# A gated linear recurrence: its inner levels in blocks of 32 tokens instead of 128 x 128 products

## The chip, the cores and the metric

The program runs on one core of a Trainium2 chip. The metric is the device time of one execution in microseconds, the median of several runs. TensorE is called PE, VectorE DVE, ScalarE ACT, GpSimd POOL, and SyncE, which issues the DMAs, SP.

## The reference, cut to what matters

The reference is a decoder trunk of two layers on 512 tokens of width 1024. Each layer is half a feed-forward step, a mixer, and half a feed-forward step. The second layer's mixer is HGRN2, a linear recurrence with a decay for each key channel, 8 heads of 128 key and 128 value channels. Its heart:

```python
q = jax.nn.silu(zq)
log_f = jnp.logaddexp(jnp.log(lbf), jnp.log1p(-lbf) + jax.nn.log_sigmoid(zf))
k = (1.0 - lbf) * jax.nn.sigmoid(-zf)
...
    bcum = jnp.cumsum(gc, axis=2)
    diff = jnp.where(causal, bcum[:, :, :, None, :] - bcum[:, :, None, :, :], -jnp.inf)
    a = jnp.einsum('bhtk,bhsk,bhtsk->bhts', qc, kc, jnp.exp(diff))
    o_intra = jnp.einsum('bhts,bhsv->bhtv', a, vc)
```

So for each head a causal matrix `a[t, s]` is wanted, the sum over channels of query t times key s times the decay between them, and the output is that matrix times the values (the state that the reference carries from chunk to chunk is the same sum for more distant tokens).

## The kernel before

The decay between two tokens can't be written as a product of one factor per token over long distances without overflow, so the kernel splits the pairs of tokens by distance. The 512 tokens are 4 chunks (`c`) of 128. Pairs in different chunks come from the six products `ai` (lines 1147 to 1155). Pairs within a chunk come from seven levels, `HL` = 64, 32, 16, 8, 4, 2, 1: at the level m a chunk is cut into blocks of 2m, and a pair belongs to the level where its key is in the first half of a block and its query in the second half of the same one. The tile `E` holds, for each level and token, the exponential of the decay between the token and the middle of its block; lines 1167 to 1173 multiply it in place by the keys in the first halves and by the queries in the second halves, one DVE instruction of 256 elements for each half (the two of the level 1 on POOL). Then PE multiplies keys by queries. The diagonal (a token with itself) has no decay.

Which products run is the point of this case. The diagonal is computed as four full products of 128 keys by 128 queries (line 1164), of which DVE keeps the diagonal by a product with the identity (line 1165), writing all of the tile `a`. The level 64 is four products of 64 by 64 (line 1177), the level 32 eight of 32 by 32 (line 1180), alternating chunk by chunk, the level 16 sixteen of 16 by 16 (line 1189), and ACT copies their blocks into `a` (lines 1181, 1183, 1191). The levels 8, 4, 2 and 1 are four products of 128 by 128 each (line 1196): almost all of their output is thrown away, and DVE picks what belongs to the level through a mask of bytes, 512 elements an instruction (line 1197). Each fp32 product is two records on PE, each a load of weights and a pass of the moving operand; such a load and pass is called a pair below. A product whose output has 32 or fewer rows uses only the columns of the array above those PSUM partitions, so products for different partitions can run beside each other.

Eight heads run one after the other, software-pipelined: while the head h is in `hgrn_pairs`, the exponentials of h + 1 are made (line 1109, 1110, 1118, 1119; `EXP_AT` says after which step), the output of h - 1 is formed (`hgrn_out`), and that of h - 2 is transposed and split for the output projection (`hgrn_ot`). PE's instructions stay in the order in which the code is written; the other engines' order is chosen by a scheduler, and each runs its own list in that order. After the last head comes the output projection: `out_proj` loads eight weight tiles `hgrn_w_out` (512 KB each) through the three buffers called `raw`, splits each into `whi` on ACT and `wlo` on DVE, and multiplies. Its PSUM banks: six for the chunks 0 to 2, one each for the transposes of the heads 6 and 7, and the last two, for the chunk 3, are those of the transposes again once `oth` and `otl` have been read from them.

## Time and profile before

| what | value |
|---|---|
| time before, median of 3 runs (lowest to highest) | 2070.39 us (2069.94 to 2071.92) |
| the profiled execution, its own time | 2072.93 us |
| its span in the trace | 2071.2 us |
| the recurrence in the trace (queries' last product to the output projection's first) | 1565.7 to 1675.7 us |
| one head in the middle of it | 13.22 us |

The span is what the trace covers, from the first instruction to the last; the execution's own time is 1.7 us longer. In the trace matmul ends are modelled, so that the durations of neighbouring matmuls overlap; what one costs in a stream is the distance from its start to the next start.

### The profile page before, as it was taken

Reading aid. Unit: us, or ns where it says so; the run is one execution under the profiler, and the core shown is the slowest. Engines: PE = TensorE matmul, PEld = TensorE weight load, DVE = VectorE, ACT = ScalarE, POOL = GpSimd, SP = SyncE. Lnnn points to the kernel's source line nnn. Section 1 sums busy time; section 2 is a strip of 40 time slices with the busy share of each in tenths; the row PEclk is TensorE's granted clock in tenths of the full one; section 3 lists DMA queues with packets and bytes.
Section 4 is the critical chain, followed back from the end, with each engine's and each line's share of the span. In section 5 each row is a group of like instructions: output and inputs, shape, how many; then the busy total and the mean of one; then the engine's idle time right before and its main releaser. Section 6 shows DMA issues by size and latency. Waiting matters only on the chain.

```text
span 2071.2 us, 34517 instructions
## 1 busy us (share of the span) xinstructions
PE 2039.3 (98%) x14265; PEld 1870.6 (90%) x14265; DVE 1402.0 (68%) x2108; ACT 987.2 (48%) x1594; POOL 196.1 (9%) x307
## 2 busy tenths in 40 slices
PE   9999999999999999999999999999999999999998
PEld 9998998978898899899899989988888989998996
DVE  8846865377775896487598568663647869945864
ACT  5543552355565355245345435534736734542551
POOL 0000002001122200000110000020321212000002
PEclk9999999999999999999999999999999999999999
DMA  5441342341101145133234413513230023442331
GB/s 183 123 146 58 103 143 74 91 111 42 31 32 52 61 123 163 41 104 112 91 102 134 142 51 103 175 51 102 88 113 32 2 72 96 128 144 62 102 123 41
DMA packets 138762, 194.00 MB, mean 94 GB/s; under 512 B 8571, under 2 KB 117435, under 8 KB 138604
## 3 DMA queue, kind: packets, MB, share of 16 engines
q1 hardware_dynamic: 138604, 191.79, 29.9%
q8 instruction: 112, 1.84, 0.4%
q14 instruction: 46, 0.38, 0.1%
HBM read 189.58 MB, written 2.19 MB: 93 GB/s over the span
## 4 chain that ended last, share of the span: by engine, by line
PE 82%; DVE 10%; ACT 3%; DMA 2%; issue 1%; POOL 1%; SPq 1%; POOLq 0%; DVEq 0%; ACTq 0%
PE ps L140 22%; PE ps L142 22%; PE ps L141 22%; PE po L860 3%; DVE wlo L124 2%; PE ps L844 2%; DVE raw L394 2%; DMA fr<-in_ffn_w_up_dram 2%; PE ps L1196 1%; PE ps L363 1%; DVE xlo L124 1%; PE sc L811 1%; PE sc L812 1%; PE ps L182 1%; DVE fr L394 1%
## 5 line engine op out<-in xcount | busy, mean ns | idle before, releaser
L124 DVE TENSOR_TENSOR wlo<-raw,whi 128x1024 fp32r<-128x1024 f32 (+1 forms) x253 | 311.4, 1235 | 259.6 <-ACT whi L123 258.7
L123 ACT ACTIVATE whi<-raw 128x1024 fp32r<-128x1024 f32 (+1 forms) x253 | 265.7, 1055 | 337.4 <-PE ps L142 152.8
L140 PE MATMUL ps<-xh,whi 128*128 128x256 f32 (+1 forms) x992 | 294.6, 297 | 1.9 <-DVE qs L754 1.3
L141 PE MATMUL ps<-xl,whi 128*128 128x256 f32 (+1 forms) x992 | 293.4, 296 | 0.7 <-DVE xl L124 0.7
L142 PE MATMUL ps<-xh,wlo 128*128 128x256 f32 (+1 forms) x992 | 293.3, 296 | 0.0
L142 PE MATMUL ps<-whi,xlo 128*128 128x512 f32 x704 | 274.4, 390 | 1.5 <-DVE xlo L124 1.5
L140 PE MATMUL ps<-whi,xhi 128*128 128x512 f32 x704 | 274.5, 390 | 0.0
L141 PE MATMUL ps<-wlo,xhi 128*128 128x512 f32 x704 | 274.0, 389 | 0.0
L140 PEld LDWEIGHTS ps<-xh,whi 128*128 128x128 f32 x992 | 186.6, 188 | 9.6 <-DVE qs L754 1.4
L141 PEld LDWEIGHTS ps<-xl,whi 128*128 128x128 f32 x992 | 186.4, 188 | 7.6 <-DVE xl L124 1.1
L142 PEld LDWEIGHTS ps<-xh,wlo 128*128 128x128 f32 x992 | 186.9, 188 | 6.4
L123 ACT ACTIVATE whi<-fr 128x1024 fp32r<-128x1024 f32 x120 | 126.1, 1061 | 115.5 <-PE ps L141 82.3
L140 PE MATMUL ps<-xh,xhi 128*128 128x256 f32 x640 | 178.0, 278 | 1.6 <-DVE c L449 1.4
L142 PE MATMUL ps<-xh,xlo 128*128 128x256 f32 x640 | 177.6, 278 | 0.0
L141 PE MATMUL ps<-xl,xhi 128*128 128x256 f32 x640 | 177.6, 278 | 0.0
L124 DVE TENSOR_TENSOR wlo<-fr,whi 128x1024 fp32r<-128x1024 f32 x120 | 145.5, 1220 | 45.8 <-ACT whi L123 45.6
L142 PEld LDWEIGHTS ps<-whi,xlo 128*128 128x128 f32 x704 | 132.1, 188 | 30.6 <-DVE xlo L124 3.2
L394 DVE TENSOR_TENSOR raw<-fr 128x1024 f32<-128x1024 f32 x120 | 145.6, 1221 | 17.7 <-DMA fr<-in_ffn_w_up_dram 16.3
L141 PEld LDWEIGHTS ps<-wlo,xhi 128*128 128x128 f32 x704 | 132.2, 188 | 27.1
L140 PEld LDWEIGHTS ps<-whi,xhi 128*128 128x128 f32 x704 | 132.2, 188 | 26.8
L124 DVE TENSOR_TENSOR xlo<-h,xhi 128x1024 fp32r<-128x1024 f32 x44 | 53.9, 1226 | 110.8 <-ACT xhi L123 110.8
L140 PEld LDWEIGHTS ps<-xh,xhi 128*128 128x128 f32 x640 | 120.4, 188 | 2.4 <-DVE c L449 2.4
(270 smaller groups left out, 4830.8 us busy)
## 6 DMA issues: line engine op xcount, KB each, us to landing
raw<-in_ffn_w_down_dram SPq DMA_DIRECT2D x88, 512.0 KB, 3.6
fr<-in_ffn_w_gate_dram SPq DMA_DIRECT2D x80, 512.0 KB, 4.0
fr<-in_ffn_w_up_dram SPq DMA_DIRECT2D x80, 512.0 KB, 5.1
raw<-in_hgrn_w_in_dram SPq DMA_DIRECT2D x32, 512.0 KB, 4.1
raw<-in_nsa_w_in_dram SPq DMA_DIRECT2D x18, 512.0 KB, 4.2
raw<-in_ffn_w_gate_dram SPq DMA_DIRECT2D x8, 512.0 KB, 5.4
raw<-in_ffn_w_up_dram SPq DMA_DIRECT2D x8, 512.0 KB, 4.6
raw<-in_nsa_w_out_dram SPq DMA_DIRECT2D x8, 512.0 KB, 3.5
```

The costliest lines, as they stand in the source:

```text
L123: a = self.nc.scalar.activation(hi, src, AF.Copy)
L124: b = self.nc.vector.tensor_tensor(lo, src, hi.bitcast(F32), op=ALU.subtract)
L140: mm(out, l[0], r[0], start=start, stop=False)
L141: mm(out, l[0], r[1], start=False, stop=False)
L142: mm(out, l[1], r[0], start=False, stop=stop)
L182: self.nc.tensor.transpose(p[:, j, :], self.x[c][:, k * P : (k + 1) * P], self.ident)
L363: nc.tensor.matmul(out, l, xx, start=k == low == 0 and xx is x[0], stop=k == 7 and low == 1)
L394: tt(out, x, y, op=op)
L811: nc.tensor.matmul(sc, l, kh[g][:, ts[0] : ts[0] + x, :n], start=True, stop=False)
L812: nc.tensor.matmul(sc, l, kl[g][:, ts[0] : ts[0] + x, :n], start=False, stop=True)
L844: nc.tensor.transpose(p[:, j * P : j * P + P], pf[:, (b0 + j) * P : (b0 + j + 1) * P], self.ident)
L860: nc.tensor.matmul(po[:, ii, t, :], pt[:, t * (i + 1) + j, :], v[j][:, t, g, :], start=j == 0, stop=j == i)
```

## The change

The diagonal and the levels 16 to 1 are computed in compact blocks of `BD` = 32 tokens: for each level sixteen products of 32 keys by the 16 queries of the same block (line 1208 of the new file), and for the diagonal sixteen of 32 by 32 (line 1172). Two levels share one PSUM bank, 64 columns each. DVE collects them in a small tile `diag` of 128 x 128 elements with masks of that form, 64 elements an instruction, and ACT copies `diag` into `a` by four instructions at the end. `a` is one of two tiles that POOL fills with zeros once. The four products of the level 64 are written in turn to the two halves of the PSUM partitions and stand together, and the eight of the level 32 behind them. At the level 1 the keys are used as they are, since their decay there is one; its queries are multiplied on DVE, and POOL multiplies nothing any more. Keys and queries of a head lie in one tile `kq`, so that one DVE instruction of 512 elements serves a level. `tot` is dropped. The tile `ai` comes from the pool `raw` instead of its own.

```diff
-ON_POOL = ((6, 0), (6, 1))
+BD = 32
...
+            eye = work.tile([P, BD], F32, name="eye")
+            for b in range(0, P, BD):
+                self.nc.gpsimd.tensor_copy(eye[b : b + BD], self.ident[b : b + BD, b : b + BD])
...
+                within = [att.tile([P, NT, P], F32, name=f"a{i}") for i in range(2)]
+                for t in within:
+                    self.nc.gpsimd.memset(t, 0.0)
...
-        tot = att.tile([P, 2], F32, name="tot", bufs=2)
-        dve.tensor_copy(tot, EI[:, 1:4:2, P - 1])
...
-        ai = att.tile([P, 6, P], F32, name="ai", bufs=2)
+        ai = self.raw.tile([P, 6, P], F32, name="ai", tag="raw")
...
+        diag = att.tile([P, NT, BD], F32, name="diag", bufs=2)
+        ps = self.psum()
+        for c, b in blocks:
+            s = slice(c * P + b, c * P + b + BD)
+            mm(ps[b : b + BD, BD * c : BD * c + BD], k[:, s], q[:, s], start=True, stop=True)
+        dve.tensor_tensor(diag, ps[:, 0 : NT * BD].rearrange(four, c=NT), eye.unsqueeze(1).to_broadcast([P, NT, BD]), op=ALU.mult)
+        other(2)
+
+        for l, m in enumerate(HL[:-1]):
+            e = E[:, l].rearrange("p c t -> p (c t)").rearrange("p (b x m) -> p b x m", x=2, m=m)
+            dve.tensor_tensor(e, e, self.ap(kq, 0, [[2 * m, T // (2 * m)], [T + m, 2], [1, m]]), op=ALU.mult)
+
+        e = E[:, 6].rearrange("p c t -> p (c t)")[:, 1::2]
+        dve.tensor_tensor(e, e, q[:, 1::2], op=ALU.mult)
...
-        for l in range(3, 7):
-            other(l + 1)
-            p = self.psum()
-            for c in range(NT):
-                mm(p[:, c * P : c * P + P], E[:, l, c, :], E[:, l, c, :], start=True, stop=True)
-            dve.copy_predicated(a, masks[:, l - 3, :].unsqueeze(1).to_broadcast([P, NT, P]), p.rearrange("p (c t) -> p c t", c=4))
+        for pair in ((2, 3), (4, 5), (6,)):
+            p, copies = self.psum(), []
+            for n, l in enumerate(pair):
+                if l > 2:
+                    other(l + 1)
+                m, at = HL[l], n * T // 2 // NT
+                e = E[:, l].rearrange("p c t -> p (c t)")
+                ev = e.rearrange("p (d b x m) -> p d b x m", d=T // BD, x=2, m=m)
+                for c, b in blocks:
+                    s, o = c * P + b, at + BD // 2 * c
+                    mm(p[b : b + BD, o : o + BD // 2], (k if m == 1 else e)[:, s : s + BD], ev[:, s // BD, :, 1, :], start=True, stop=True)
...
+                copies.append(partial(dve.copy_predicated, to, mask, p[:, at : at + T // 2 // NT].rearrange("p (c b m) -> p c b m", c=NT, m=m)))
+            for f in copies:
+                f()
+        for b in range(0, P, BD):
+            act(a[b : b + BD, :, b : b + BD], diag[b : b + BD], AF.Copy)
```

On PE, in the middle of one head, before: the last products of the level 32, the level 16, exponentials of the next head (lines 1118 and 1109), the levels 8, 4 and 2, exponentials, the level 1.

```order
L1180 MATMUL ps<-E 32x32 x2
L1189 MATMUL ps<-E 16x16 x16
L1118 MATMUL ps<-sums,hl 128x128 x2
L1118 MATMUL ps<-sums,hl 128x256 x2
L1109 MATMUL pa<-sums,hl 128x448 x2
L1196 MATMUL ps<-E 128x128 x12
L1109 MATMUL pa<-sums,hl 128x448 x2
L1196 MATMUL ps<-E 128x128 x4
```

And in the changed kernel, from the diagonal to the last level (line 1126 is the old 1118, 1117 the old 1109):

```order
L1172 MATMUL ps<-kq 32x32 x16
L1117 MATMUL pa<-sums,hl 128x448 x2
L1186 MATMUL ps<-E 64x64 x4
L1190 MATMUL ps<-E 32x32 x8
L1208 MATMUL ps<-E 32x16 x16
L1126 MATMUL ps<-sums,hl 128x128 x2
L1126 MATMUL ps<-sums,hl 128x256 x2
L1117 MATMUL pa<-sums,hl 128x448 x2
L1208 MATMUL ps<-E 32x16 x48
L1117 MATMUL pa<-sums,hl 128x448 x2
L1208 MATMUL ps<-E,kq 32x16 x16
```

The exponentials of the next head stand at the same places between the levels as before; what stands between them are now runs of 16 to 48 small products.

On SP, from the last loads of the queries' weights to those of the next feed-forward step, before:

```order
L132 DMA raw<-in_hgrn_w_in_dram 128x4x256 x4
L132 DMA raw<-in_hgrn_w_out_dram 128x1024 x7
L211 DMA hlg<-in_ln_gain_dram 128x1024
L212 DMA hlb<-in_ln_bias_dram 128x1024
L132 DMA raw<-in_hgrn_w_out_dram 128x1024
L132 DMA raw<-in_ffn_w_gate_dram 128x4x256 x2
```

And in the changed kernel:

```order
L133 DMA raw<-in_hgrn_w_in_dram 128x4x256 x4
L133 DMA raw<-in_hgrn_w_out_dram 128x1024 x4
L212 DMA hlg<-in_ln_gain_dram 128x1024
L213 DMA hlb<-in_ln_bias_dram 128x1024
L133 DMA raw<-in_hgrn_w_out_dram 128x1024 x4
L133 DMA raw<-in_ffn_w_gate_dram 128x4x256 x2
```

The loads have the same order but for three that stand behind `hlg` and `hlb`; but `raw` now belongs to eight tiles `ai` first, one for each head, and a load waits for PE's last use of one of them.

On DVE, from the last head's use of its output (`zg`) to the first normalisation of the output projection, before:

```order
L1216 SCALAR_TENSOR_TENSOR zg_14318<-ps,ry,zg_14318 128x128
L124 TENSOR_TENSOR wlo<-raw,whi 128x1024 x5
L124 TENSOR_TENSOR otl<-ps,oth 128x512 x2
L124 TENSOR_TENSOR wlo<-raw,whi 128x1024 x3
L229 SCALAR_TENSOR_TENSOR x_71<-x_71,ps 128x512
```

And in the changed kernel (one more `wlo`, that of the first output weight, stands ahead of the last two heads' `zg`):

```order
L1234 SCALAR_TENSOR_TENSOR zg_14310<-ps,ry,zg_14310 128x128
L125 TENSOR_TENSOR wlo<-raw,whi 128x1024 x6
L125 TENSOR_TENSOR ot<-ps,ot 128x512
L125 TENSOR_TENSOR wlo<-raw,whi 128x1024 x2
L125 TENSOR_TENSOR ot<-ps,ot 128x512
L125 TENSOR_TENSOR wlo<-raw,whi 128x1024 x3
L230 SCALAR_TENSOR_TENSOR x_71<-x_71,ps 128x512
```

Four more splits of weights stand here, and the split of the head 7's transposed output is behind all eight output weights and the first one of the feed-forward step.

## Rows read from the trace of the kernel before

**Rows 1.** the profile's page, part 1: engine, busy time, share of the span, instructions.

```profile
PE 2039.3 (98%) x14265; PEld 1870.6 (90%) x14265; DVE 1402.0 (68%) x2108; ACT 987.2 (48%) x1594; POOL 196.1 (9%) x307
```

**Rows 2.** busy time by stretch, columns in line one; last: one head.

```profile
core 0: us, PE busy (x) PEld busy (x) DVE busy (x) ACT busy (x) POOL busy (x), PEclk, DMA share, GB/s
1566.00:1571.00 5.00, 3.21 (x18) 2.39 (x16) 0.80 (x3) 4.97 (x8) 0.00 (x0) 1.00 0.33 105
1571.00:1576.00 5.00, 4.66 (x24) 4.47 (x24) 4.53 (x11) 3.64 (x7) 2.08 (x2) 0.66 0.00 0
1576.00:1581.00 5.00, 5.00 (x81) 4.34 (x80) 4.27 (x10) 4.24 (x11) 0.00 (x0) 1.00 0.01 3
1636.06:1649.28 13.22, 13.22 (x150) 12.41 (x150) 11.95 (x29) 8.60 (x24) 3.42 (x5) 1.00 0.01 1
```

**Rows 3.** chain of waits, that head, 13.22 us: shares by line.

```profile
by line: PE ps L1196 27.0%; PE pa L1109 12.2%; PE ps L1154 10.5%; PE ps L1208 10.1%; PE ps L1118 8.1%; PE ps L1177 7.8%; PE ps L1209 6.8%; PE ps L1164 6.7%; PE ps L1180 5.4%; PE ps L1222 3.3%; PE ps L1189 2.0%
```

**Rows 4.** order of time, PE, head before: start, us, line, op, shape, records.

```profile
1626.27 0.33 PE L1177 MATMUL ps<-E 128*64 128x64 f32 x2
1626.53 0.26 PE L1180 MATMUL ps<-E 128*32 128x32 f32 x4
1627.93 0.42 PE L1189 MATMUL ps<-E 128*16 128x16 f32 x29
1628.28 0.73 PE L1118 MATMUL ps<-sums,hl 128*128 128x128 f32 x4
```

**Rows 5.** source lines, PE's sequencer: ns, first and last start (us).

```profile
L1189 PEldq EVENT_SEMAPHORE  x1: 51/51/51, 1627.0 to 1627.0; - x1
L1196 PEldq EVENT_SEMAPHORE  x1: 51/51/51, 1628.5 to 1628.5; - x1
```

**Rows 6.** groups by line, the head of Rows 3: count, busy us, mean ns.

```profile
L1197 DVE COPY_PREDICATED a<-masks,ps 128x512 f32<-128x512 uint8 x4 | 3.0, 742 | 0.0
L1173 DVE TENSOR_TENSOR E<-E,qt 128x256 f32<-128x256 f32 x6 | 2.5, 417 | 0.0
L1165 DVE TENSOR_TENSOR a<-ps,ident 128x512 f32<-128x512 f32 x1 | 0.7, 679 | 0.0
L1139 DVE COPY tot<-EI 128x2 f32<-128x2 f32 x1 | 0.2, 169 | 0.6 <-ACT EI L1119 0.6
L1183 ACT ACTIVATE a<-ps 32x128 f32<-32x128 f32 x2 | 0.5, 260 | 0.0
L1191 ACT ACTIVATE a<-ps 16x64 f32<-16x64 f32 x4 | 0.9, 215 | 0.1
```

**Rows 7.** order of time: DMA issues, DVE and PE around the projection's start.

```profile
1530.02 35.46 SPq L132 DMA_DIRECT2D raw<-in_hgrn_w_out_dram  x7
1682.12 1.51 SPq L132 DMA_DIRECT2D raw<-in_ffn_w_gate_dram  x2
raw<-in_hgrn_w_out_dram SPq DMA_DIRECT2D x7, 512.0 KB, 3.5
1678.70 1.13 DVE L1216 SCALAR_TENSOR_TENSOR zg<-ps,ry,zg 128x128 f32<-128x128 f32 x4 [1.16 <-POOL ry L219]
1679.75 3.48 DVE L124 TENSOR_TENSOR wlo<-raw,whi 128x1024 fp32r<-128x1024 f32 x3
1689.62 1.28 DVE L124 TENSOR_TENSOR otl<-ps,oth 128x512 fp32r<-128x512 f32 x2
1675.67 0.23 PE ps L140
1684.04 0.44 PE ps L1222 x4
1688.66 0.44 PE ps L1222 x4
```

**Rows 8.** line 1154, first head (order of time) and later one (chain).

```profile
1571.35 2.82 PE L1154 MATMUL ps<-qi,ki 128*128 128x128 f32 x12 [0.43 <-DVE ki L1143]
1636.47 1.39 PE ps L1154 x12
```

More of the change, by code (lines that the diff above doesn't have):

```diff
@@ L930, in hgrn_body @@
         w = self.a["hgrn_w_in"][0]
-        kt, qt, xh, xl = [], [], [], []
-        for _ in range(NK):
-            kt.append(pool.tile([P, T], F32, name="kt", tag="kq", bufs=2 * NK))
-            qt.append(pool.tile([P, T], F32, name="qt", tag="kq", bufs=2 * NK))
+        xh, xl = [], []
+        kq = [pool.tile([P, 2, T], F32, name="kq", tag="kq", bufs=NK) for _ in range(NK)]
+        kt, qt = ([t[:, i] for t in kq] for i in range(2))
         zg = [pool.tile([P, D], F32, name=f"zg{c}") for c in range(NT)]
@@ L941, in hgrn_body @@
             sums = work.tile([P, NSUM], F32R, name="sums")
-            masks = work.tile([P, 4, P], U8, name="masks")
+            masks = work.tile([P, 5, BD], U8, name="masks")
+            eye = work.tile([P, BD], F32, name="eye")
+            for b in range(0, P, BD):
+                self.nc.gpsimd.tensor_copy(eye[b : b + BD], self.ident[b : b + BD, b : b + BD])
             with ExitStack() as e2:
@@ L967, in hgrn_body @@
                         *nxt, side = self.hgrn_exps(att, right, self.hgrn_split(parts, h + 1, lf), sums)
-                    last, cur = cur, self.hgrn_pairs(att, h, exps, kt, qt, masks, side)
+                    last, cur = cur, self.hgrn_pairs(att, within[h % 2], exps, kq[h], masks, eye, side)
                     if h > 1:
@@ L1076, in hgrn_proj @@
             pool.tensor_tensor(z3, z3, gn.unsqueeze(1).to_broadcast([P, 4, P]), op=ALU.mult)
-        raw = self.raw.tile([P, 4, P], I32, name="raw", tag="raw")
+        raw = self.raw.tile([P, 5, BD], I32, name="raw", tag="raw")
         nc.sync.dma_start(raw, self.a["masks"])
@@ L1122, in hgrn_exps, with hgrn_pairs @@
         return E, EI, [partial(within, n) if n < NT else partial(across, n - NT, far[n - NT]) for n in EXP_ORDER]
-    def hgrn_pairs(self, att, h, exps, kt, qt, masks, side):
+    def hgrn_pairs(self, att, a, exps, kq, masks, eye, side):
         nc = self.nc
         act, dve, mm = nc.scalar.activation, nc.vector, nc.tensor.matmul
-        k, q = kt[h], qt[h]
+        k, q = kq[:, 0], kq[:, 1]
         E, EI = exps
@@ L1157, in hgrn_pairs @@
         other(1)
-        a = att.tile([P, NT, P], F32, name="a", bufs=2)
-        af = a.rearrange("p c t -> p (c t)")
+        blocks = [(c, b) for c in range(NT) for b in range(0, P, BD)]
+        four = "p (c t) -> p c t"
+        diag = att.tile([P, NT, BD], F32, name="diag", bufs=2)
[4 more added lines that the diff above has]
+        dve.tensor_tensor(diag, ps[:, 0 : NT * BD].rearrange(four, c=NT), eye.unsqueeze(1).to_broadcast([P, NT, BD]), op=ALU.mult)
@@ L1181, in hgrn_pairs @@
-        act(a[0:64, :, 64:128], p[0:64, 0:256].rearrange("p (c t) -> p c t", c=4), AF.Copy)
+                mm(p[b : b + 32, 128 + 32 * c : 160 + 32 * c], el[:, b : b + 32], el[:, b + 32 : b + 64], start=True, stop=True)
+        for o in range(2):
+            act(a[0:64, o::2, 64:128], p[64 * o : 64 * o + 64, 0:128].rearrange("p (c t) -> p c t", c=2), AF.Copy)
         for b in (0, 64):
-            act(a[b : b + 32, :, b + 32 : b + 64], p[b : b + 32, 256:384].rearrange("p (c t) -> p c t", c=4), AF.Copy)
+            act(a[b : b + 32, :, b + 32 : b + 64], p[b : b + 32, 128:256].rearrange(four, c=NT), AF.Copy)
@@ L1265, in hgrn_consts @@
     tau, j = np.arange(P)[:, None], np.arange(P)[None, :]
-    masks = [(tau // (2 * m) == j // (2 * m)) & (tau % (2 * m) < m) & (j % (2 * m) >= m) for m in HL[3:]]
+    tau, j = tau % BD, j[:, :BD]
+    masks = [(tau // (2 * m) == j // (2 * m)) & (tau % (2 * m) < m) & (j % (2 * m) >= m) for m in HL[2:]]
     return np.concatenate([sums, sums]), np.stack(masks, 1).astype(np.int32)
```

35 lines of the change are left out of this document (9 added, 26 removed).

## The prediction, made before the changed kernel ran

> **What bounds the kernel now.** I read the page first: PE is busy for 98% of the span [rows 1]. Since the change touches one stage, I went on to the stretches of that stage, then to the chain of waits of one head, then to the order of time on PE within it. At the front of the recurrence PE is idle for a while (3.21 of 5.00 us) and its granted clock falls to 0.66 in the next 5 us; from then on PE is busy throughout, one head taking 13.22 us [rows 2]. In that head DVE is busy for 11.95 us and ACT for 8.60 [rows 2], so DVE is a close second. The chain of that head is PE from end to end: no other engine has a share in it [rows 3]. So a head costs what its products cost on PE, and what the change takes from PE there comes off the time, down to where DVE, ACT or PE's own supply of instructions is next.
>
> **What goes from PE.** The lines that the change rewrites are 1196 (27.0%), 1177 (7.8%), 1164 (6.7%), 1180 (5.4%) and 1189 (2.0%) of the head's chain [rows 3]: 48.9% of 13.22 us, 6.46 us. The other 6.76 us stay as they are. Line 1196 alone is 32 pairs in 3.57 us, 0.11 us for each.
>
> **What comes instead.** Per head 32 pairs for the diagonal, 8 for the level 64, 16 for the level 32 and 5 x 32 for the levels 16 to 1: 216 pairs, where there were 96. What does one cost? There are two answers in the trace, and they differ by three times.
>
> The array's answer: the level 16 is already done so, and 29 of its records start between 1627.93 and 1628.28, where the next line starts [rows 4]: 12 ns each, since four groups of columns work side by side. 216 such pairs would take 2.6 us.
>
> The sequencer's answer: PE's sequencer executes some waits itself, and these have times of their own. One stands ahead of the level 16, at 1627.0, another ahead of the level 4, at 1628.5 [rows 5]. Between them the program has 32 pairs of the level 16, 6 of exponentials and 8 of the level 8: 46 pairs in 1.5 us, 33 ns each. From the first product of the level 64 (1626.27, [rows 4]) to the wait at 1627.0 there are 24 pairs: 30 ns each. Both are ceilings, as a wait may have held it, but two agreeing ones look like a rate. So the fast level 16 above ran from instructions that were already queued, and a long run of small products has to be paid at about 30 ns a pair: 216 x 30 = 6.5 us, no gain at all, less what is queued when a run begins.
>
> How much is queued? The 216 pairs come in four runs: the diagonal (32), the levels 64 to 16 (56), 8 to 2 (96) and 1 (32). Ahead of each stand long products, in which the sequencer gains: 0.41 us or more of line 1109 for two pairs (12.2% of the head for eight [rows 3]), enough to issue some 13, so some 11 ahead; ahead of the third also half of line 1118 (8.1%), 0.94 us for 6 pairs, some 25 ahead; ahead of the first also line 1154 (10.5%, 1.39 us), so that its 32 may all be queued. Then the runs pay 0 + 45 + 71 + 21 = 137 pairs at 30 ns, 4.1 us, and the first 32 pairs the array's price, 0.4 us: **4.5 us**. That is my value, nearer to the sequencer's end because its two readings are of this very place; the bounds are 2.6 us (all queued) and 7.1 us (216 x 33 ns, none queued). A head saves 6.46 - 4.5 = 2.0 us (between 3.9 and -0.6), **eight heads 15.8 us**.
>
> The Trainium skill has a rule against such a change: TensorEngine Tiling, section Instruction Overhead, gives each matmul an overhead of about 60 cycles, so that a dimension that is already small is no use to tile. At 2.4 GHz I estimate 25 ns a pair from it, 5.4 us a head and 8.5 us in all instead of 15.8. The 12 ns of [rows 4] are under it, the sequencer's 30 to 33 ns [rows 5] are over it, so the trace doesn't bear it out as a floor, but it points the same way.
>
> **DVE and ACT.** DVE loses 4 x 0.74 us of masked copies and gets five of 64 elements; the trace has none so small, and I bound one by 0.17 us (line 1139, two elements) and 0.42 (line 1173, 256 elements), nearer to the first; five are 0.85 to 2.1, I take 1.2. The diagonal falls from 0.68 to 0.3 by the same bounds, `tot` (0.17) goes. The twelve products of 256 elements at 0.42 become six of 512 (line 1165 has that size: 0.68) and one of 256: about 4.5 for 5.0 us [all rows 6]. In sum about 11.95 - 2.8 = 9.1 us. ACT gets one more copy of 128 elements and, for four copies of 64 (0.215 each), four of 128 (line 1183: 0.26): about +0.5 us on 8.60 [rows 2, 6]. Both lie below the 6.76 + 4.5 = 11.3 us that PE then takes; they are the floor if PE is faster than I think. POOL's two products per head leave it with nothing on the path, and the copies, zeros and masks made once lie beside queries' products.
>
> **The price at the other end.** Before, seven of the eight output weights are loaded from 1530 on, under the queries' products [rows 7], and four of them are split there. Now the buffers `raw` serve `ai`, so the first weight waits for the head 5's `ai`, the others for the heads 6 and 7 and for each other. SP's queue behind them holds `hlg`, `hlb` and the feed-forward step's weights. Let t0 be the projection's first product (1675.67 now, [rows 7]). A weight lands 3.5 us after its issue and a split on DVE takes 1.16 [rows 7]. The first weight is there in time: its buffer is free before the last head's products. The second is issued when the first is split, some 3 us before t0, but its `wlo` stands on DVE behind the last `zg`, which ends at t0 + 4.1 (1679.8, [rows 7]); so it is ready at t0 + 5.3 and PE wants it at t0 + 4.4, after one weight's 18 products of 0.233 us, 36 of them lie between 1675.67 and 1684.04: **0.9 us**. The third and fourth follow at 1.16 us each and are wanted 4.2 us apart. The next four go around the buffers: each is issued when an earlier one is split, at about t0 + 5.4, 6.6, 7.8 and 11.4, and the feed-forward's first behind them at t0 + 13.3; that one lands near t0 + 17.5 and its split ends near t0 + 20. Behind it on DVE stands the split of the head 7's transposed output, which frees the last PSUM bank, at about t0 + 21. PE wants that bank for the chunk 3 at t0 + 17.5 now (second transposes 1688.66 plus 0.44 and 18 products), t0 + 19.3 then, with the 0.9 us and one bank's three products: **1.9 us**. Now it is free at 1690.9, in time [rows 7]. Together 2.8 us lost, between 0 (if the loads land earlier) and 6 (if each lands 2 us later).
>
> **Sum.** Profiled execution: 2072.9 - 15.8 + 2.8 = 2059.9 us. The median of the runs is 2.5 us below the profiled one, and I take that off: **2057 us**.
>
> **Rivals.** First, *the array decides*: the sequencer is faster than its two waits show, and small products run near 12 ns. PE would then need 9.4 us a head, and DVE's and ACT's 9.1, which wait for PE in turn, hold it at about 10: 8 x 3.2 = 25.6 saved, less 2.8: 2048 us. For it: [rows 4]; against it: that two intervals give the same rate.
>
> Second, *another engine sets the pace*: DVE and ACT each serve a head in an order of their own, and the masked copies now come in pairs after two levels; at 12.5 us a head PE saves 0.7 x 8 = 5.8, less 2.8: 2067 us. For it: DVE is busy for 11.95 of 13.22 us now; against it: it loses the most work of all.
>
> Third, on the other side, *the sequencer has nothing in hand*: its waits for PSUM banks and for DVE stand at the head of each run, and if each holds it until PE has run dry, all 216 pairs cost 33 ns: 7.1 us for 6.46, +0.7 a head, with the loss at the end 2070.4 + 5.3 + 2.8 = 2078 us. It decides from 30 ns a pair on, with nothing queued. For it: a wait stands ahead of nearly every run; against it: at 1627.0 the sequencer was 14 pairs ahead, since PE came to the level 16 at 1627.9. The Trainium skill (TensorE: Matmul & The Clock Gate, section Wait - 56ns, not 53.3ns?) knows a slower one still, 62 ns for a matmul where the sequencer's program does the decoding, which I estimate at 13.4 us of small products a head and 2129 us in all. The 46 pairs in 1.5 us [rows 5] took half of that each, so it has no chance of its own beside this rival's.
>
> Fourth, *the clock falls*: behind the idle stretch at the start the granted clock was 0.66, between its levels of 1.2 and 2.4 GHz, and line 1154 took 2.82 us for 1.39 [rows 2, 8]. If PE starved between small products were taken for idle, the 6.76 us of long products would double: +6.8 - 2.0 = 4.8 a head, 38 + 2.8 us, 2111 us; it eats the gain from 1.3 times the length on. For it: [rows 8]; against it: the small products of now, 15% of the head by lines 1177, 1180 and 1189, leave the clock at 1.00 [rows 2]. The Trainium skill (the same page, section What's actually happening) says that the gate is held open by PE's activity, which agrees with [rows 2]; whether sparse small products count as such no row here shows.
>
> **How the numbers follow.** Forecast 0.60, the array decides 0.14, another engine 0.10, the sequencer with nothing in hand 0.10, the clock 0.06. A measurement of this kernel tells about 0.2%, 4.1 us, from no change. Faster: 0.57 of the forecast's 0.60, all of the first rival and half of the second, 0.76; the same: the rest of these but for a little, and a part of the third near zero, 0.11; slower 0.13. The range leaves out the clock and most of the third rival: 2046 to 2069 us, which takes in the bounds of the end's loss and most of those of the small pairs.
>
> **What would show it.** A head near 11.3 us on PE in the middle of the recurrence; line 1208's records some 30 ns apart in the run of the levels 8 to 2, with PE's loader idle for no wait on another engine; at 12 ns the first rival holds, and at 33 with the runs' first pairs late the third. DVE and ACT near 9 us a head, with waits for PE. At the projection two stops of PE, one for `wlo` after 18 products, one for a bank ahead of the chunk 3, released by DVE. Granted clock 1.00 from 1576 on; a head with less is the fourth rival. I am wrong if a head takes over 12.7 us, or if PE stops for over 6 us at the projection.

## The result, and the profile after

The changed kernel takes 2059.15 us (median of 4 runs, 2055.03 to 2061.76) for 2071.15 us before: a ratio of 0.994, 95% interval 0.992 to 0.9959, so 0.4 to 0.8% faster. The forecast was 2057 us. Its profiled execution took 2055.03 us, before 2072.93.

The two traces, cut at the same places on PE (the starts of queries' last product, of the output projection's first and of the next feed-forward step's first), give this:

| stretch, us | before | after | difference | forecast |
|---|---|---|---|---|
| from the start to queries' last product | 1565.33 | 1560.71 | -4.6 | 0 |
| recurrence | 110.10 | 94.55 | -15.55 | -15.8 |
| output projection | 46.88 | 50.12 | +3.24 | +2.8 |
| the rest | 348.9 | 347.8 | -1.1 | 0 |

The 4.6 us of the first stretch are there by 1043 us, in the layer before, of which the change touches nothing (the same transposes start at 1048.3 us before and at 1043.7 after). In the traces of all kernels of this study the stretch ends between 1560.7 and 1566.6 us, without order; so one profiled time is uncertain by some 6 us, and below the kernels are compared by the length of the recurrence and of the projection.

The page's line of busy times (part 1), which answers to [rows 1]:

```profile
PE 2009.6 (98%) x15225; PEld 1834.5 (89%) x15225; DVE 1379.1 (67%) x2068; ACT 990.1 (48%) x1602; POOL 183.0 (9%) x297
```

PE has 960 pairs more and 30 us less to do. What became of four heads in the middle, the third to the sixth before and the fourth to the seventh after, shows in windows (the columns: length, busy time and count of PE, PE's loader, DVE, ACT and POOL, the granted clock, DMA), first before, then after:

```profile
1596.37:1649.53 53.16, 53.16 (x594) 49.75 (x594) 48.69 (x119) 37.94 (x104) 13.79 (x20) 1.00 0.01 2
```

```profile
1599.40:1644.45 45.05, 41.13 (x1071) 34.35 (x1071) 37.04 (x95) 39.04 (x106) 6.81 (x12) 1.00 0.01 3
```

Before, PE is busy all of the 53.16 us, 13.29 a head. After, a head takes 11.26 us, and PE is idle for 3.92 of the 45.05; DVE and ACT are busy for 9.26 and 9.76 us of a head. The forecast of 11.3 us is met, but by a mean of unequal heads: the third to the seventh took 13.36, 13.37, 13.22, 13.22 and 12.81 us before and take 12.12, 11.80, 11.53, 11.23 and 10.49 after. (The third to the sixth, as in the window of before, take 11.67 us each after, 10.5 of them busy on PE.) Why they get shorter one after the other was not tried. And PE is no longer all that the head waits for. The waits of PE in the same four heads say for whom it stopped (engine, operation, line and what released it: us in total, times, longest), PE first, then its loader:

```profile
PE ps L1126 <- DVE zg L1234: 2.3, 4, 0.8
PE ps L1172 <- ACT EI L1127: 0.8, 3, 0.5
PE ps L1160 <- DVE ot L125: 0.4, 1, 0.4
PE ps L1227 <- DVE diag L1213: 0.3, 1, 0.3
```

```profile
PEld ps L1126 <- DVE zg L1234: 2.7, 4, 0.9
PEld ps L1208 <- issue: 2.4, 8, 0.3
PEld ps L1172 <- ACT EI L1127: 1.9, 3, 0.8
```

And the order of time on PE in one of them (start, length, what; in brackets the idle time before it; lines 1117 and 1126 are the exponentials, the old 1109 and 1118):

```profile
1625.61 0.68 PE L1117 MATMUL pa<-sums,hl 128*128 128x448 f32 x2
1626.22 0.45 PE L1186 MATMUL ps<-E 128*64 128x64 f32 x8
...
1626.87 0.44 PE L1208 MATMUL ps<-E 128*32 128x16 f32 x30
1627.81 0.73 PE L1126 MATMUL ps<-sums,hl 128*128 128x128 f32 x4 [0.51 <-DVE zg L1234]
1628.38 0.57 PE L1117 MATMUL pa<-sums,hl 128*128 128x448 f32 x2
1628.88 1.03 PE L1208 MATMUL ps<-E 128*32 128x16 f32 x96
1629.84 0.68 PE L1117 MATMUL pa<-sums,hl 128*128 128x448 f32 x2
1630.45 0.45 PE L1208 MATMUL ps<-E,kq 128*32 128x16 f32 x32
1630.82 0.66 PE L1240 MATMUL ps<-ident,zg 128*128 128x128 f32 x4
```

The run of 96 small pairs (levels 8 to 2) goes from 1628.88 to 1629.84, 10 ns a pair with the change to the next line; the last of the 96 starts 0.846 us after the first, 8.9 ns a pair. The prediction had 30 ns for most of them. Where PE's own work got so much shorter than forecast, the head did not: it now goes round in a ring over the other engines. The chain of waits of one head (in order of time: start, length, what; with "..." where "issue" and shorter pieces of the same engines are left out) has no PE in it from the squares of one head to those of the next:

```profile
1612.70 0.88 ACT lf L1230 x6
...
1613.66 0.30 POOL ss L1231
...
1614.34 1.05 POOL ry L220
...
1615.41 1.13 DVE zg L1234 x4
1616.54 0.20 DVE diag L1173
1616.73 0.33 DVE E L1181
...
1617.80 0.70 DVE hl L1104
...
1618.52 0.56 DVE qi L1148
...
1620.64 0.31 DVE diag L1213
...
1620.97 0.31 ACT a L1215
...
1622.27 0.60 ACT ot L124
...
1623.92 0.88 ACT lf L1230 x6
```

Squares on ACT, the root on POOL, `zg` on DVE; behind it in DVE's list the next head's diagonal, level 1, split, `qi`, masked copies; then ACT's copies of `diag`, and behind them in ACT's list the squares again. From 1612.70 to 1623.92 that is 11.22 us, and the head that PE does next, the sixth, takes 11.23. [rows 3], the chain of before, was PE alone.

This is not every head. In the two behind it ACT waits for PE's outputs before the squares (waits from 1600 to 1645), and the profile follows the chain no further than 1626.6; so PE is part of the way again there.

```profile
ACT lf L1230 <- PE ps L1227: 0.9, 2, 0.6
```

At the end, the two stops that were forecast (waits of PE from 1655 to 1706):

```profile
PE ps L141 <- DVE ot L125: 1.8, 1, 1.8
PE ps L142 <- DVE wlo L125: 0.9, 1, 0.9
```

### The profile page after: what moved, and what is told of

It reads as the page before. It is cut to its first block, busy times and chain, and to the rows that moved or that the text cites. A ratio compares the mean times of both kernels' runs of the same rounds, so it can differ in the third digit from the quotient of the medians.

```text
span 2053.2 us, 36367 instructions
## 1 busy us (share of the span) xinstructions
PE 2009.6 (98%) x15225; PEld 1834.5 (89%) x15225; DVE 1379.1 (67%) x2068; ACT 990.1 (48%) x1602; POOL 183.0 (9%) x297
## 3 DMA queue, kind: packets, MB, share of 16 engines
q8 instruction: 119, 1.95, 0.4%
## 4 chain that ended last, share of the span: by engine, by line
PE 81%; DVE 10%; ACT 4%; issue 3%; POOL 1%; DMA 1%; POOLq 0%; SPq 0%; DVEq 0%; ACTq 0%
PE ps L141 23%; PE ps L143 23%; PE ps L142 23%; PE po L861 3%; DVE wlo L125 2%; PE ps L364 2%; PE ps L845 2%; DVE raw L395 1%; PE sc L812 1%; PE sc L813 1%; PE ps L183 1%; DMA fr<-in_ffn_w_up_dram 1%; DVE xlo L125 1%; ACT whi L124 1%; DVE xl L125 1%
## 5 line engine op out<-in xcount | busy, mean ns | idle before, releaser
L125 DVE TENSOR_TENSOR wlo<-raw,whi 128x1024 fp32r<-128x1024 f32 (+1 forms) x253 | 311.3, 1234 | 243.6 <-ACT whi L124 242.9
```

The costliest lines, as they stand in the source:

```text
L125: b = self.nc.vector.tensor_tensor(lo, src, hi.bitcast(F32), op=ALU.subtract)
```

## The experiments

All of them change the kernel after, but for the last. The recurrence and the projection are those of each profiled run; the ratio is to the kernel before, with its 95% interval.

| kernel | ratio | recurrence | projection | last head |
|---|---|---|---|---|
| before | 1 | 110.10 | 46.88 | 13.09 |
| after | 0.994 (0.992 to 0.9959) | 94.55 | 50.12 | 10.81 |
| one more instruction on POOL | 0.9946 (0.9929 to 0.9964) | 98.01 | 49.65 | 12.66 |
| outputs ahead of transposes | 0.9952 (0.9931 to 0.9974) | 99.13 | 49.41 | 15.40 |
| copies of `diag` on POOL | 0.9933 (0.9919 to 0.9947) | 92.32 | 49.73 | 11.36 |
| `zg` later in DVE's list | 0.9925 (0.9907 to 0.9942) | 89.12 | 50.09 | 10.16 |
| these two and a shorter root | 0.9931 (0.9918 to 0.9945) | 88.33 | 49.98 | 10.55 |
| levels 8 to 2 three times, in place | 1.0173 (1.0152 to 1.0193) | 141.94 | 52.28 | 17.31 |
| three times, by whole levels | 1.018 (1.0161 to 1.0199) | 141.74 | 53.32 | 18.37 |
| twice, by whole levels | 1.0068 (1.0049 to 1.0087) | 114.77 | 52.99 | 12.90 |
| `ai` in its own tile | 0.996 (0.9945 to 0.9975) | 99.08 | 48.00 | 15.18 |
| ring and end | 0.9912 (0.9894 to 0.993) | 92.56 | 47.74 | 14.60 |
| the same, last copies on ACT | 0.9897 (0.9878 to 0.9916) | 87.56 | 50.94 | 9.77 |
| before, with `zg` later | 1.0012 (0.9998 to 1.0027) | 112.75 | 46.95 | 15.08 |

A head's length below is the distance between the first products of line 1160 of two heads, all on PE.

**Is there a ring, and who is in it?** The first edit makes POOL's part longer:

```diff
+        pool.tensor_scalar(ss, ss, 1.0, None, op0=ALU.mult)
         pool.tensor_scalar(ss, ss, 1.0 / P, None, op0=ALU.mult)
```

> The changed kernel with one more instruction on POOL per head, a multiplication of `ss` (128 x 4) by 1 ahead of the reciprocal root; it is 0.3 to 0.8 us on POOL. Theory of the loop: the pace of a head is set by squares on ACT, root on POOL, `zg` on DVE, the PSUM bank that this frees, the exponentials across chunks and the rest of the head's products on PE up to the next squares; then the recurrence gets longer by about 0.4 to 0.7 us for each of some six heads, 2.5 to 4.5 us in all. Rival, PE's own supply of small products sets the pace (the prediction's): nothing, since POOL is idle for 8.5 us of a head.

The third to the seventh head took 12.12, 11.80, 11.53, 11.23 and 10.49 us in the changed kernel and take 12.14, 12.08, 11.86, 11.51 and 10.80 here: +0.3 us in each of four, which is what the added instruction costs POOL (0.30 us for line 1231 in the chain above). POOL is idle for over 8 us of a head, and still its instruction counts in full. The sum is smaller than I expected, 1.2 us, as it is four heads and not six; the rest of the longer recurrence is the first head (+0.7), the second (-0.3) and the last (+1.85), where PE's granted clock was 0.63 to 0.69 for 5 us. In the whole time it is lost in the spread.

The second edit shortens PE's way to the squares and touches nothing else:

```diff
-                    if h > 1:
-                        self.hgrn_ot(pool, h - 2, zg, xh, xl)
                     if h:
                         self.hgrn_out(h - 1, *last, v, zg, lf)
+                    if h > 1:
+                        self.hgrn_ot(pool, h - 2, zg, xh, xl)
```

> The changed kernel with the outputs of the head before issued ahead of the transposes instead of behind them, nothing else. Theory of the loop: the squares start 0.49 us (the four transposes on PE) earlier, the bank comes free earlier by as much, and a head gets shorter by up to 0.49 us while PE stops for that bank: 2 to 3.5 us off the recurrence of 94.6 us. Rival, PE's own supply of small products sets the pace: nothing, as PE has the same instructions.

I had drawn the ring through PE then (by the bank that `zg` frees), and that was wrong: the heads are 12.15, 11.89, 11.51, 11.22 and 10.49 us, those of the changed kernel within 0.1 and three of them within 0.02. PE's waits move from `zg` to `EI` of line 1127, and the length stays. So these 0.49 us on PE are not in the ring; the chain of waits above, ACT to POOL to DVE to ACT, is the one that fits both runs. The last head lost 4.6 us: the projection's first product waited 4.2 us for a `zg`.

The third edit takes work out of ACT's part:

```diff
-            act(a[b : b + BD, :, b : b + BD], diag[b : b + BD], AF.Copy)
+            nc.gpsimd.tensor_copy(a[b : b + BD, :, b : b + BD], diag[b : b + BD])
```

> The changed kernel, but the four copies of `diag` into `a` run on POOL instead of ACT. They are 1.25 us of ACT per head and stand in ACT's list ahead of the squares, and ACT waits up to 0.5 us in a head for the masked copies in front of them. Theory that the lists of ACT, DVE and POOL set the pace (a ring: squares, root, `zg`, then DVE's list, masked copies, ACT's copies, squares): 0.5 to 1.2 us less in each of five or six heads, 3 to 7 us off the recurrence (94.6 us in the profiled run of the changed kernel). Theory that PE's supply of instructions sets the pace: the recurrence stays within 1 us.

The heads: 11.77, 11.10, 11.12, 10.81 and 10.37, 0.1 to 0.7 us shorter; the recurrence 2.2 us shorter, under the 3 to 7 expected. The fourth fills the time in which DVE waits for POOL:

```diff
-        dve.tensor_tensor(e, e, q[:, 1::2], op=ALU.mult)
+        done = dve.tensor_tensor(e, e, q[:, 1::2], op=ALU.mult)
+        if scale:
+            with self.after([first, done]):
+                scale()
```

Here `scale` is the loop of line 1234 for the head before and `first` the diagonal's product (line 1173).

> The changed kernel, but `zg` of a head is put behind the diagonal's product and the level 1's product of the next head in DVE's list, which now stand behind it and wait with it; DVE is idle for 1.2 to 1.6 us there, until POOL's root is done. Theory of the ring: 0.7 us of DVE's work moves into that idle time, so a head gets shorter by up to 0.7 us, and the recurrence by 3 to 4.5 us. Theory that PE's supply sets the pace: the recurrence stays within 1 us.

The recurrence is 5.4 us shorter. Of these, 1.1 us are the first head's (8.76 us for 9.85), over which the granted clock was 1.00 in this run and 0.87 in the changed kernel; they can't be put down to the edit. The other 4.3 us lie within the 3 to 4.5 expected. The waits of DVE from 1595 to 1645, in the changed kernel and in this one:

```profile
DVE zg L1234 <- POOL ry L220: 6.2, 4, 1.8
```

```profile
DVE zg L1240 <- POOL ry L220: 2.5, 4, 0.7
```

The heads: 12.09, 10.64, 10.72, 10.65 and 9.64; 0.6 to 1.2 us less in four of five. Both edits and a root with one instruction less on POOL together:

```diff
-        pool.tensor_scalar(ss, ss, 1.0 / P, None, op0=ALU.mult)
-        r = self.rsqrt(ss, NT, RMS_EPS)
+        r = self.small.tile([P, NT], F32, name="ry", tag=f"ry{NT}")
+        pool.tensor_scalar(r, ss, 1.0 / P, float(RMS_EPS), op0=ALU.mult, op1=ALU.add)
+        pool.tensor_tensor(r, r, self.mhalf[:, :NT], op=ALU.pow)
```

> The changed kernel with the copies of `diag` on POOL, `zg` behind the diagonal and the level 1 in DVE's list, and POOL's two instructions ahead of the root made one (0.3 us less of POOL per head, what one more of them cost in the run with an added one). Theory of the ring: the three add up to 1.5 to 2 us a head, as far as PE's own need of about 10 us a head, so that heads of 10.5 to 11.8 us come to about 10.2 and the recurrence to 87 to 89 us; the whole some 6 to 8 us under the changed kernel, near 2052. Theory that PE's supply sets the pace: within 2 us of the changed kernel.

Heads of 11.00, 10.12, 10.73, 10.31 and 9.64, the recurrence 88.33 us, 6.2 less than in the changed kernel; DVE's wait for the root is down to 0.3 us:

```profile
DVE zg L1241 <- POOL ry L1237: 0.3, 1, 0.3
```

The gains don't add up (2.2 and 4.3, without that first head, are already more than 6.2), since PE's own work, 10.28 us busy in a head of the changed kernel, is reached. The chain of waits from 1611 to 1645 goes over PE's lines again first of all:

```profile
by line: PE ps L1212 12.7%; PE pa L1118 12.0%; PE ps L1230 11.9%; PE ps L1231 8.0%; PE ps L1127 7.5%; DVE E L1179 7.4%; ACT lf L1234 7.1%; DVE hl L1105 6.1%; PE ps L1249 5.2%; PE ps L1161 4.1%; POOL ry L1237 4.0%; issue 2.8%; ACT E L1119 2.
```

The median of 2055.45 us is 3 us above what was expected.

**Was the ring there before the change?** The control is the edit that gained most, in the kernel before:

```diff
+        if scale:
+            with self.after([first, done]):
+                scale()
```

Here `done` is the last of the levels' products on DVE and `first` the diagonal's; the four instructions of `zg` are `scale`.

> The kernel before the change, with `zg` of a head behind the diagonal's product and the last of the levels' products on DVE, the edit that took 5.4 us off the recurrence of the changed kernel. Theory that PE alone set the pace before the change, and the ring only after it: nothing, the recurrence stays at 110.1 us within 1 us, heads at 13.2. If the ring had a share before: heads get shorter.

Heads of 13.57 to 13.61 us for 13.22 to 13.37, so nothing is gained, and some 0.3 us a head is lost. The recurrence, 112.75 us, is 2.65 us longer where at most 1 was expected: PE now stops for 0.24 us a head for the diagonal's product on DVE, and for 1.9 us ahead of the projection for a `zg`; and this although the first head is 1.6 us shorter, at a granted clock that did not fall there. What was worth over 4 us behind the change is worth nothing ahead of it. The control is a weak one, since DVE waited for POOL's root for only 1.5 us in 50 there (6.2 in the changed kernel), so there was less to gain; the stronger sign is that PE was busy in all of the 53.16 us above. PE set the pace there, as [rows 3] says.

**What does a small product cost?** The products of the levels 8 to 2 are issued three times, first each one three times in a row, then by whole levels.

```diff
-                    mm(p[b : b + BD, o : o + BD // 2], (k if m == 1 else e)[:, s : s + BD], ev[:, s // BD, :, 1, :], start=True, stop=True)
+                    for _ in range(3 if 2 < l < 6 else 1):
+                        mm(p[b : b + BD, o : o + BD // 2], (k if m == 1 else e)[:, s : s + BD], ev[:, s // BD, :, 1, :], start=True, stop=True)
```

> The changed kernel, but every product of the levels 8, 4 and 2 is issued three times, 192 pairs more in a head, so that the run between two exponentials of `within` is 288 pairs long. The prediction's theory, the sequencer's 30 ns a pair: +5.8 us a head, +46 us in all. The array's price as the trace of the changed kernel shows it, 96 pairs in 0.85 us, 8.8 ns each: +1.7 us a head, +13.5 us in all, and the run of 288 in 2.5 us. If the first 96 come from a queue and the rest at the sequencer's rate, something between, and the records' distance changes within the run.

```diff
-                for c, b in blocks:
+                for c, b in blocks * (3 if 2 < l < 6 else 1):
```

> As the run with every product of the levels 8 to 2 three times, but here the sixteen products of a level are repeated as a whole, so that neighbours always use different columns of the array (there the same columns came three times in a row, 15 ns a pair). The array's price is then the 8.8 ns of the changed kernel: 288 pairs in 2.5 us, +1.7 us a head, +13.5 us in all. The other theory: instructions are fetched in blocks of 16 KB, and in the run before two fetches never started less than 3.5 us apart, 3.8 us on the whole; if a block is 256 instructions, 128 pairs, then a long run costs 29.7 ns a pair whatever the array does: a run of 288 in 5 us or more, with stops of 1 to 2 us in it, and again some +46 us in all.

Both recurrences are 47 us longer, 47.2 us / 1536 added pairs = 30.7 ns a pair, although in the first the pairs of a run are some 15.5 ns apart and in the second 8.7. So the array doesn't decide it. The order of time on PE in one run of 288 of the second:

```profile
1605.29 0.97 PE L1208 MATMUL ps<-E 128*32 128x16 f32 x92
1606.91 1.30 PE L1208 MATMUL ps<-E 128*32 128x16 f32 x128 [0.65 <-issue]
1610.65 1.15 PE L1208 MATMUL ps<-E 128*32 128x16 f32 x68 [2.45 <-issue]
```

After a stop of 0.65 us, so with nothing in hand, 128 pairs run through, 8.7 ns each; then PE stops for 2.45 us, waiting for no other engine. So the sequencer can issue a pair every 9 ns, and it stops after 128 of them. The page of the changed kernel counts a DMA queue of instructions (queue, kind: packets, MB, share of 16 engines):

```profile
q8 instruction: 119, 1.95, 0.4%
```

1.95 MB / 119 = 16.4 KB a packet, and that kernel has 2 x 15225 instructions on PE and its loader, 256 for each packet: 128 pairs. From 1561 to 1705 us the queue has 10 packets before the change, 18 after and 29 in this run. Here they start 3.4 us apart at the least, 3.7 on the mean within the bursts, and each takes about 1 us. 128 pairs in 3.7 us are 29 ns a pair, the rate at which a long run is supplied. All of PE's stops for it in the recurrence, in the changed kernel and here:

```profile
PE ps L1208 <- issue: 1.6, 3, 0.9
```

```profile
PE ps L1208 <- issue: 26.5, 16, 2.8
```

That 29 lies so near to the 30.7 ns is in part chance, since the 47.2 us are not these stops alone. Cut by the starts on PE, 19.9 us are more idle time (25 more in stops for instructions, 5 less in other waits), 17.7 are the added pairs themselves, and 9.6 are products that the edit doesn't touch and that took longer. (In the run with three in a row the same 47 us are 7.0, 33.7 and 6.7.) The granted clock was 0.50 for 37.6 us of this recurrence and for 3.4 of the changed kernel's; behind the stop of 2.45 us:

```profile
1610.60:1614.60 4.00, 3.95 (x108) 3.33 (x109) 1.59 (x5) 1.69 (x4) 0.00 (x0) 0.50 0.02 4
```

So the price of a long run is that of bringing its instructions, of the pairs, and of the clock that is lost behind the stops; no run held the clock fixed to part them further.

The Trainium skill (Runtime: NRT & Kernel Launch, section Instruction fetch mechanics) describes such blocks of 16 KiB, 256 instructions, and says that crossing into the next one is mostly hidden. The size agrees with the count above; that it is hidden holds for the products of before, which need a block in some 11 us, but not for these runs, with their stops of 2.45 us.

The last of these runs has them twice:

```diff
-                for c, b in blocks:
+                for c, b in blocks * (2 if 2 < l < 6 else 1):
```

> The changed kernel with the sixteen products of each of the levels 8, 4 and 2 issued twice, 96 pairs more in a head (with three times, 192 pairs more, the recurrence got 47 us longer, 31 ns a pair). If every added pair costs what the supply of instructions costs: +2.9 us a head, +23 us. The array's price: +0.85 us a head, +7 us. If the ring hides what the supply leaves idle: a head has about 550 instructions on PE in the changed kernel, 740 here, that is 2.9 blocks of 256 at 3.8 us, 11.0 us, about the ring's 10.5 to 11.8; then the first 96 pairs cost less than the second, some 8 to 16 us.

20.2 us / 768 = 26 ns a pair: the price is paid almost from the first added pair (12.8 of the 20.2 us are more stops for instructions, and the granted clock was 0.50 for 10.2 us). That on the mean the blocks would come in time (11.0 us a head) doesn't help, since the pairs come in bursts: 192 of them want more than one block within 2 us. The run of 96 in the changed kernel is under one block.

**The end.** `ai` gets its own tile again, and `qi` (2 KB a partition for 3, free earlier) takes its place in `raw`:

```diff
-        qi = att.tile([P, 4, P], F32, name="qi", bufs=1)
+        qi = self.raw.tile([P, 4, P], F32, name="qi", tag="raw")
...
-        ai = self.raw.tile([P, 6, P], F32, name="ai", tag="raw")
+        ai = att.tile([P, 6, P], F32, name="ai", bufs=2)
```

> The changed kernel, but `ai` has a tile of its own again and the smaller `qi`, which is free some 9 us before the recurrence ends, takes its place in `raw`. The prediction's theory of the end: both stops of PE at the output projection come from the late weight loads, so they go; from the projection's first product to the feed-forward step's first it takes about 46.9 us as before the change (50.1 in the changed kernel), 3.2 us less. Some of it may come back in the recurrence, where three or four weights are now split (1.2 us on DVE each): up to 2 us. Rival: the stops have another cause (the splits on DVE behind the last head's `zg`), the stretch stays near 50 us.

The projection is 2.1 us shorter of 3.2 expected, so the stops do hang on the late loads; a stop of 0.9 us is left, for a `zg`. But the last head is 4.4 us longer, where up to 2 were expected, since the splits of three weights stood between its masked copies on DVE. Next, with the edits of the ring, the splits are put behind these copies; `tail` holds the last head's last masked copy and ACT's last copy of the level 32:

```diff
-            self.out_proj(self.a["hgrn_w_out"][0], gb, wl, xh, xl, late)
+            with self.after(self.tail):
+                self.out_proj(self.a["hgrn_w_out"][0], gb, wl, xh, xl, late)
```

> The version with the three edits of the ring together, and for the end: `ai` in a tile of its own again, `qi` in `raw` instead, and the splits of the output weights put behind the last head's masked copies in DVE's list and behind its copies of the level 32 in ACT's (in the run with `ai` in its own tile three of these splits stood between the masked copies of the last head and made it 15.2 us for 10.8). Theory of the end as in the prediction: three weights are split before the last `zg`, so PE's stop for the second weight's `wlo` goes and the one for the chunk 3's bank gets shorter; the projection to the feed-forward step's first product takes 47 to 48 us for 50.0, the last head stays below 11.5. Recurrence and projection together 135 to 137 us (138.3 in the version with the three edits, 144.7 in the changed kernel); the whole about 2 us less than that version, 2052 to 2053.

The projection took 47.74 us as expected, the heads up to the last 9.6 to 11.3, and the last 14.60 instead of below 11.5, so that both stretches together are 140.3 us and not 135 to 137. POOL's copies are the reason: its order of time, the wait of PE behind it, and the stretches with the granted clock in the third column from the right:

```profile
1647.46 4.11 POOL L1221 COPY a<-diag 32x128 f32<-32x128 f32 x4 [2.70 <-DVE diag L1219]
```

```profile
PE ps L1233 <- POOL a L1221: 2.7, 1, 2.7
```

```profile
1645.00:1648.00 3.00, 2.66 (x72) 2.43 (x61) 2.73 (x10) 2.95 (x5) 0.54 (x1) 1.00 0.16 63
1648.00:1651.00 3.00, 0.93 (x9) 0.73 (x7) 3.00 (x4) 1.99 (x9) 2.88 (x4) 0.99 0.52 158
1651.00:1654.00 3.00, 2.38 (x11) 2.39 (x12) 1.44 (x5) 0.00 (x0) 1.76 (x3) 0.50 0.83 255
1654.00:1657.00 3.00, 3.00 (x14) 2.81 (x14) 0.10 (x1) 0.65 (x5) 0.00 (x0) 0.50 0.30 116
```

The four copies took 1.03 us each on the mean, while DVE split weights and weights landed beside them (DMA share 0.52); the 17 others from 1600 us on took 0.56. Which of the two slowed them was not tried. PE stopped for 2.7 us, and behind the stop its granted clock was 0.50 for 6 us, the lower of its two levels: two pairs of the outputs take 0.43 us there and 0.22 in the head before.

```diff
-            nc.gpsimd.tensor_copy(a[b : b + BD, :, b : b + BD], diag[b : b + BD])
+            if final:
+                self.tail[1] = act(a[b : b + BD, :, b : b + BD], diag[b : b + BD], AF.Copy)
+            else:
+                nc.gpsimd.tensor_copy(a[b : b + BD, :, b : b + BD], diag[b : b + BD])
```

> The version with the edits of the ring and of the end, but the last head's copies of `diag` are again ACT's. In the run before, POOL took 1.03 us for each of the four there (0.3 us on ACT), PE stopped for 2.7 us behind them, and its granted clock was 0.50 in the 6 us behind the stop, so that the last head took 14.6 us. Without that stop: last head near 10.5 us at a clock of 1.00, recurrence 88.4 us, projection 47.7: 136.1 us together (144.7 in the changed kernel, 157.0 before), some 4 us less than the run before, 2049 to 2050 us.

The last head took 9.77 us at a clock of 1.00, the recurrence 87.56. But the projection is back at 50.94 us, with a stop for the last bank and the clock at 0.83 behind it:

```profile
PE ps L141 <- DVE ot L125: 2.2, 1, 2.2
```

```profile
1670.00:1680.00 10.00, 7.76 (x28) 5.88 (x27) 4.59 (x5) 4.79 (x6) 0.00 (x0) 0.83 0.50 155
```

Recurrence and projection are 138.5 us, not the 136.1 expected, and its 2054.42 us (median of 4, 2048.75 to 2055.77) not the 2049 to 2050. Its ratio of 0.9897 (0.9878 to 0.9916) is the best, below that of the changed kernel with intervals that don't overlap. So both kernels are beaten, by 1.0 and 0.4%. Why the stop for the last bank was there with this order and not with the one before it was not tried.

## Why the prediction was right, and where it was not

**What bounds the kernel now: right.** PE alone: it was busy in all of the four heads of before, and the control without gain fits.

**What goes from PE: right.** By the starts, the rewritten lines took 6.3 us of a head in the four heads of before, for 6.46 forecast. PE's busy time, 53.16 us before and 41.13 after, doesn't show it at once, as the second holds the new pairs.

**What comes instead: wrong in its price, and by a wrong reason.** I took 4.5 us a head from the sequencer's 30 to 33 ns. Of the 45.05 us of four heads, lines 1172, 1186, 1190 and 1208 have 13.5 (start to next start), of which 2.3 are the stops ahead of line 1126: 2.8 us a head for the 216 pairs, near the array's 2.6 and far from my 4.5. The failing step is that two waits of the sequencer [rows 5] "look like a rate". They don't: with nothing in hand it issues a pair in 8.7 ns, and the sign that was named, records of line 1208 some 30 ns apart, came out at 8.9. The trace of before tells whose rate the 33 ns were. At the first wait the sequencer was 14 pairs ahead of PE; at the second, at 1628.46, it was 12 ahead: two of line 1118 [rows 4], two of line 1109 and the first eight of line 1196.

```profile
1628.85 0.56 PE L1109 MATMUL pa<-sums,hl 128*128 128x448 f32 x2
1629.25 2.84 PE L1196 MATMUL ps<-E 128*128 128x128 f32 x24
```

So it moved 46 pairs while PE itself started 48: the reading is the pace of a PE at work, behind which it stood. Of the 24 pairs of the other reading PE had itself started 10 by then, and the rest are the 14 ahead. That an added pair costs 30.7 ns is the same number from other causes, the blocks of 128 pairs and the clock behind the stops, and it doesn't hold for the runs of up to 96 of this change. The 25 ns a pair that I estimated from the Trainium skill (TensorEngine Tiling, section Instruction Overhead) are not what these pairs cost either.

**What PE does besides: missed.** The "other 6.76 us stay" was a little low: the exponentials of line 1117 took 9.4 us in four heads without the stops behind them, 7.86 before, as the small products start 0.3 us after the last of them; and the head that I took as a model was itself 0.2 us below the mean of four in these lines.

**DVE and ACT: sizes right, conclusion wrong.** Masked copies took 0.25 us each (1.25 for five, I had 1.2), the products of 512 elements 0.68, the diagonal 0.28; DVE is 9.26 us busy (9.1 forecast), ACT 9.76 (9.1). But "both lie below" a PE of 11.3 us only spoke of busy time. PE needs 10.28 us, DVE and ACT 9.3 and 9.8, and ACT, POOL and DVE wait for each other in a ring that takes 11.2 in the head followed above. That was my second rival, *another engine sets the pace*, at a chance of 0.10, with a head of 12.5; the first, *the array decides*, had the small pairs right and held the head at "about 10". What happened is the first rival's price and the second's reason, and together they make the forecast's number. The head of 11.26 us was right by luck, by two errors that cancel: 1.7 us too much for the pairs, against 0.98 us of stops and 0.7 us in the other lines that I did not have.

**The price at the other end: right.** Two stops, 0.9 us for the second weight's `wlo` after 18 products and 1.8 for the last bank, behind the split of the head 7 on DVE; 0.9 and 1.9 were forecast, and the projection is 3.24 us longer for 2.8. That the late loads are the cause of most of it is shown by the run with `ai` in its own tile, which got 2.1 of it back.

**The sum: right.** -15.55 + 3.24 us for -15.8 + 2.8; the profiled time of 2055.03 us has another 4.6 us from ahead of the recurrence, where nothing was changed, and the median of 2059.15 is 2 us above the forecast. The term of the recurrence is right by the luck of the head.

**The other rivals.** *The sequencer with nothing in hand* did not come about; in the runs of 192 and 288 pairs an added pair cost 26 and 31 ns, near its 33, but by stops between blocks that run at 9 ns. *The clock* stayed at 1.00 from 1571 on through recurrence and projection in the profiled run; in the run with POOL's copies at the end it was 0.50 behind a stop of PE of 2.7 us, and in the run of 288 pairs for 37.6 us in all, so the rival's loss is real where PE stops often; the longest stop of the change there, 1.8 us, was not followed by it. (In the run with each product three times in a row, stops of 1.2 to 1.9 us were.)

## What to carry to other kernels

A busy engine that loses a quarter of its work hands the pace to whatever is next, and that may be no engine but a ring of lists: look for the chain that goes from an instruction back to the same instruction of the round before, since each microsecond in it counts in full, even on an engine that is idle for most of the time. A wait's time on a sequencer says when it got there, not how fast it can go: ask how far it stood ahead of its engine at both ends, and for a rate take a run that starts behind a stop. Count instructions in bursts: in these traces more than 128 pairs in a row want a second block of instructions 1.1 us after the first (8.7 ns a pair), and it comes some 3.7 us after it. And compare the granted clock of two runs, stretch by stretch, before a difference is put down to an edit.

## What the runs showed of the hardware

Products of 32 keys by 16 queries cost 8.9 ns a pair when neighbours use different columns and some 15.5 ns when three in a row use the same. In the run of 288 pairs PE stopped for up to 2.8 us between blocks of 256 instructions. POOL's copy of 32 x 128 elements took 0.56 us, and 1.03 beside DVE's splits of 1024 elements and the landing of weights. Behind a stop of 2.7 us PE's granted clock was 0.50 for 6 us.
